# A two-layer decoder trunk: q, k and v of the attention layer in blocks of 512 columns, one block of tokens after the other, instead of units of 256 columns for both blocks at once

## The chip, the cores and the metric

The kernel runs on one core of one Trainium2 chip. The metric is the device time of one execution in microseconds. The kernel before was run three times: 932.15, 935.91 and 936.04 us, median 935.91 us. One more execution was recorded by the profiler.

## The reference

The input is one sequence of 256 tokens with 1024 features, in float32. Two layers follow each other. Only the first half of layer 0, its attention, is touched by the change:

```python
qkv = (h @ w_qkv).reshape(B, S, 3 groups, 3 (q, k, v), 16 heads, 64)    # h = rms_norm(x)
q = rms_norm(qkv[:, :, :, 0], q_gain)      # per head, over its 64 features
k = rms_norm(qkv[:, :, :, 1], k_gain)
v = qkv[:, :, :, 2]
for each group g with (window, dilation) in (128, 1), (512, 4), (2048, 16):
    s   = q . k * scale - slope * distance     # causal, keys gathered by stride
    lse = logsumexp(s);  out_g = exp(s - lse) . v
o = sum over groups of softmax(lse)_g * out_g
x = x + o @ w_o
```

After it come a squared-ReLU MLP (1024 to 4096 to 1024), an embedding gate, and layer 1: an mLSTM mixer, another MLP and another gate. The projection to q, k and v has 9216 output columns: 3 groups times (q, k, v) times 16 heads of 64.

## The kernel before, in words

**Weights.** All weights come as a stream of units, arrays of [128, 2048] float32 (1 MB). `dma(u)` loads unit u into one of three raw buffers from SyncE's queue. Float32 precision is reached with three products of a faster 32-bit type: each weight chunk of 512 columns is split into a high part `hi` (a rounding copy on ScalarE, L166) and a low part `lo` (raw minus hi on VectorE, L167), the activations are split in the same way (`hh`, `hl`), and each product is made as hi·hh + lo·hh + hi·hl, three matmuls into one sum. There are 12 chunk buffers each for `hi` and `lo`, which is three units.

**Slots.** A unit is worked off in four slots. `open_slot` issues the load of the unit four ahead at the first slot of a unit, and the splits of weight chunks up to `LS` = 11 slots ahead; `close_slot` calls what was registered for this slot with `at(slot, f, ...)`, the small work that is strewn between the stream's matmuls. From the code written in this order a scheduler with priorities makes the final order of each engine; splits are written at a lower priority (`BACK`), so that they move behind other work.

**q, k, v.** There are 36 units: for each quarter `qt` (four heads), for each group `g`, one unit each for q, k and v (`ty` 0, 1, 2). A unit holds 8 k-tiles of 256 columns. The activations are the stationary operand: for each k-tile and each block `b` of 128 tokens there are three matmuls of 128x256 (L474, L475, L476), so 12 matmuls in a slot, 48 in a unit and 1728 in all. The two token blocks lie side by side in one bank of 512 columns in `acc`.

**Norms of q and k.** After a q or k unit `qk_stats` squares the bank on ScalarE (`sqh`, L417) and sums over the 64 features of a head on VectorE (`ss`, L423, two instructions). After the k unit `qk_norm` makes 1/rms by an iteration of small VectorE instructions (`vqk` L427, then ten on `fqk` and `rt`, L267 to L271) and scales the sums into `n0` and `n1` (L435, four instructions). `TQ` = 5 and 6 slots later `qk_turn` transposes them on TensorE (L445, four each into `tp`), and ScalarE copies them out as `t0g` (q) and `t1g` (k), with a low part for group 0 on VectorE. So a turn of q stands behind the following v unit's four slots and one more. The second norm of the program is that of group 1 of quarter 0.

**Attention.** After the nine units of a quarter `attend` registers the quarter's attention from one slot later on: `scores` (L509 for group 0, L515 for groups 1 and 2) into `sc`, softmax on VectorE and ScalarE (L522 to L530), `turn` (L534) and `values` (L552, L556), with a step of `ST0` = 4 slots, and `ST1` = 1 for the last quarter, which falls into the stream that follows (`proj`, L317 to L319).

**The start.** x is loaded in four pieces between the pieces of the first two units. `first_stats` (L366, L368 and the iteration at L267 to L271) computes the norms of the tokens of x; some small products of the mLSTM's block matrices (`contract`, L397 to L404) run on GpSimd as soon as their input `rep` has come.

Of the kernel before, what the change touches and what calls it, by code (L numbers as in the profile page):

```python
# [32 lines left out]
# token order of layer 0: position a*64 + b*16 + c holds token 16c + 4b + a,  # L33
# which makes every class of a dilation (mod 4, mod 16) a run of positions
# [4 lines left out]

def _blocks(no, ks, singles=0):  # L40
    """outputs worked on together (k outermost): pairs, the last ones alone"""
    n = no - singles
    os = [(o, o + 1) for o in range(0, n, 2)] + [(o,) for o in range(n, no)]
    return [(b, list(ks)) for b in os]

# [57 lines left out]
def _consts():  # L103
# [5 lines left out]
    # columns: all keys for group 0; the keys of the row's class mod 4 for groups 1 and 2  # L109
    # (2 and 1 in the odd classes)  # L110
# [19 lines left out]
def _build(ctx, tc, nc, a):  # L130
# [45 lines left out]
    LS, LD = 11, 4  # L176
    fill = {}
    clock = [0]
    ahead = [7]
    LV = 6  # L180
# [5 lines left out]
    # slots after z0: the gates' steps; the start of a head, and its steps after that  # L186
    GT, HS, HO = (4, 6, 7), (6, 12, 18, 24), (0, 2, 5, 7)
    ST0 = 4
    ST1 = 1
    TQ = 5  # L190
# [35 lines left out]
    # the tensor engine's clock rises only after some time of work  # L226
# [11 lines left out]
    class Stats:  # L238
        """sum over features of x^2 -> per token"""
# [47 lines left out]
    def rstd_rows(st, power):  # L287
        """1/rms (power 1) or its square (power 2), on every partition"""
# [15 lines left out]
    def stream(blocks, rhs, done, defer=0):  # L304
        """acc[o] = sum over k of W[k, o]^T act[k]; done(outputs, acc) after every block"""
# [26 lines left out]
    # ================= layer 0: attention =================  # L332
# [47 lines left out]
    # small products of the mLSTM's block matrices  # L380
# [6 lines left out]
    def small_products():  # L387
# [4 lines left out]
        def contract(out, w, name, n, add=None):  # L392
# [22 lines left out]
    def qk_stats(qt, g, ty, acc):  # L415
        sq = atp.tile([P, 2, 4, HD], F32, name="sqh")
        act(sq, acc.rearrange("p b (h d) -> p b h d", d=HD), AF.Square)  # L417
        if ty == 0:
            STAT["ss"] = atp.tile([P, 2, 2, 4], F32, name="ss", bufs=2)
            STAT["q"] = acc  # L420
        ss = STAT["ss"]
        for b in range(2):
            dve.tensor_reduce(ss[:, b, ty], sq[:, b], axis=AX.X, op=ALU.add)  # L423

    def qk_norm(qt, g, accq, acck, ss):
        v = atp.tile([P, 2, 8], F32, name="vqk", bufs=2)
        dve.scalar_tensor_tensor(v, ss.rearrange("p b t h -> p b (t h)"), 1.0 / HD,  # L427
                                 epsx[:, :, None].to_broadcast([P, 2, 8]), op0=ALU.mult, op1=ALU.add)
        f = atp.tile([P, 2, 8], F32, name="fqk", bufs=2)
        rsqrt(f, v, [P, 2, 8])  # L430
        out = []
        for ty, acc in ((0, accq), (1, acck)):
            n = atp.tile([P, 2, 256], F32, name=f"n{ty}")
            for b in range(2):
                dve.tensor_tensor(n[:, b].rearrange("p (h d) -> p h d", d=HD),  # L435
                                  acc[:, b].rearrange("p (h d) -> p h d", d=HD),
                                  f[:, b, 4 * ty:4 * ty + 4, None].to_broadcast([P, 4, HD]), op=ALU.mult)
            out.append(n)
        return out

    def qk_turn(qt, g, ty, n):
        ps = pst.tile([P, 2, S], F32, name="tp")
        for pair in range(2):
            for b in range(2):
                nc.tensor.transpose(ps[:, pair, b * P:(b + 1) * P], n[:, b, pair * P:(pair + 1) * P], ident)  # L445
# [14 lines left out]
    def qkv_unit(qt, g, ty):  # L460
        if qt == 0 and ty == 0:
            acc = pss.tile([P, 2, 256], F32, name="sc")
        else:
            acc = psa.tile([P, 2, 256], F32, name="acc")
        for c in range(4):
            u, _ = open_slot()
            for k in (2 * c, 2 * c + 1):
                wh, wl = weights(u, k * 256, 256)
                for b in range(2):
                    if (g, ty) == (2, 2):  # L470
                        hh, hl = (t[:, k] for t in hW) if b else (t[:, k, 64:192] for t in hA)
                    else:
                        hh, hl = (t[:, k, b * P:(b + 1) * P] for t in hA)
                    mm(acc[:, b], hh, wh, start=(k == 0 and b == 0), stop=False, skip_group_check=True)  # L474
                    mm(acc[:, b], hh, wl, start=False, stop=False, skip_group_check=True)  # L475
                    mm(acc[:, b], hl, wh, start=False, stop=(k == 7), skip_group_check=True)  # L476
            if c == 3:
                if ty < 2:
                    qk_stats(qt, g, ty, acc)
                if ty == 1:  # L480
                    n = qk_norm(qt, g, STAT["q"], acc, STAT["ss"])
                    at(clock[0] + TQ, qk_turn, qt, g, 0, n[0])
                    at(clock[0] + TQ + 1, qk_turn, qt, g, 1, n[1])
                if ty == 2:
                    if g == 0:
                        VT[qt, 0] = atp.tile([P, 2, 256], F32, name="v0", bufs=2)
                    if g == 1:
                        VT[qt, 1] = atp.tile([P, 4, 256], F32, name="v12", bufs=2)
                    for b in range(2):
                        if g == 0:  # L490
                            act(VT[qt, 0][:, b], acc[:, b], AF.Copy, scale=rx[:, b:b + 1])
                            continue
                        c = 2 * b + (g == 2)
                        for r, c4 in ((slice(0, 64), c), (slice(64, 128), (c + 1) % 4)):
                            n = b + 2 * (g == 2)
# [559 lines left out]
```

## Time and profile before

| what | value |
|---|---|
| time, median of 3 | 935.91 us |
| span of the profiled execution | 933.2 us (what lies around the span isn't recorded) |
| TensorE busy | 917.9 us, 98% |
| VectorE busy | 664.5 us, 71% |
| ScalarE busy | 570.8 us, 61% |
| GpSimd busy | 41.6 us, 4% |
| DMA | 150.35 MB, mean 161 GB/s |
| chain that ended last | TensorE 92%, VectorE 5%, ScalarE 1%, DMA 1% |

The span goes from the first to the last instruction of the profiled execution. Engines are PE (TensorE matmuls), PEld (its weight loads, which overlap the matmuls), DVE (VectorE), ACT (ScalarE), POOL (GpSimd) and SP (SyncE). A matmul's record lasts longer than the time until the next one starts, since matmuls are pipelined; the pace is read from start to start. The first matmul of q, k and v starts 6.74 us after the span's start, the last one at 267.55 us, and the first matmul of the next stream (`proj`) at 273.46 us; what follows is 660 us long and isn't touched by the change, except that line numbers move by 14 or so.

### The profile page before, as it was taken

How to read it: one execution, taken by the hardware profiler on the slowest of the kernel's cores; microseconds unless marked ns; L12 is line 12 of the kernel's file. 1: busy time of each engine (PE TensorE's matmuls, PEld its weight loads, DVE VectorE, ACT ScalarE, POOL GpSimd, SP SyncE). 2: the span in 40 equal slices, each digit the busy share in tenths (PEclk: the TensorE clock that was granted, in tenths of full speed). 3: DMA queues.
4: the chain of work that ended last, by engine and by line, in shares of the span. 5: the costliest groups of instructions: out<-in, count | busy, mean ns of one | idle time of the engine just before them, and what ended most of it. 6: DMA issues, size and time to landing. Idle time of an engine off the chain costs nothing.

```text
span 933.2 us, 19379 instructions
## 1 busy us (share of the span) xinstructions
PE 917.9 (98%) x7788; PEld 899.8 (96%) x7788; DVE 664.5 (71%) x1457; ACT 570.8 (61%) x1055; POOL 41.6 (4%) x77
## 2 busy tenths in 40 slices
PE   8989999999999999999999999999999999999998
PEld 8989999999989999999999989999999999999997
DVE  6977767767756876665666987667898666656664
ACT  6646666666656666654554777668776666645542
POOL 0420000000000000000000153000000000000000
PEclk8999999999999999999999999999999999999999
DMA  8744334444342365555555343342356455555521
GB/s 297 267 144 173 136 137 139 145 165 142 137 147 92 137 211 188 186 183 182 181 181 182 131 151 136 112 147 80 115 176 211 176 182 185 187 183 185 186 105 46
DMA packets 23130, 150.35 MB, mean 161 GB/s; under 512 B 2560, under 2 KB 3200, under 8 KB 5632
## 3 DMA queue, kind: packets, MB, share of 16 engines
q1 hardware_dynamic: 23040, 149.12, 44.8%
q8 instruction: 61, 1.00, 0.4%
q14 instruction: 29, 0.24, 0.1%
HBM read 148.06 MB, written 1.05 MB: 160 GB/s over the span
## 4 chain that ended last, share of the span: by engine, by line
PE 92%; DVE 5%; ACT 1%; issue 1%; DMA 1%; SPq 0%; ACTq 0%
PE acc L317 21%; PE acc L318 20%; PE acc L319 20%; PE acc L474 6%; PE acc L475 6%; PE acc L476 6%; DVE lo L167 2%; PE tp L534 1%; PE sc L509 1%; PE tp L445 1%; PE sm L552 1%; PE sc L515 1%; PE tp L725 1%; PE tp L735 1%; PE sc L866 1%; PE sc L743 1%
## 5 line engine op out<-in xcount | busy, mean ns | idle before, releaser
L167 DVE TENSOR_TENSOR lo<-raw,hi 128x512 fp32r<-128x512 f32 x552 | 379.0, 693 | 184.5 <-ACT hi L166 182.3
L166 ACT ACTIVATE hi<-raw 128x512 fp32r<-128x512 f32 x552 | 341.9, 628 | 266.6 <-PE acc L318 208.8
L317 PE MATMUL acc<-hh,hi 128*128 128x256 f32 x640 | 184.0, 288 | 0.3 <-ACT hh L284 0.2
L318 PE MATMUL acc<-hl,hi 128*128 128x256 f32 x640 | 181.5, 284 | 0.1
L319 PE MATMUL acc<-hh,lo 128*128 128x256 f32 x640 | 181.4, 283 | 0.0
L474 PE MATMUL acc<-hi,hh 128*128 128x256 f32 x496 | 145.0, 292 | 0.0
L318 PE MATMUL acc<-hidl,hi 128*128 128x256 f32 x512 | 144.9, 283 | 0.0
L317 PE MATMUL acc<-hidh,hi 128*128 128x256 f32 x512 | 144.9, 283 | 0.0
L319 PE MATMUL acc<-hidh,lo 128*128 128x256 f32 x512 | 144.9, 283 | 0.0
L475 PE MATMUL acc<-lo,hh 128*128 128x256 f32 x496 | 140.3, 283 | 0.4 <-DVE lo L167 0.4
L476 PE MATMUL acc<-hi,hl 128*128 128x256 f32 x496 | 140.3, 283 | 0.0
L317 PEld LDWEIGHTS acc<-hh,hi 128*128 128x128 f32 x640 | 122.4, 191 | 1.5 <-issue 0.7
L318 PEld LDWEIGHTS acc<-hl,hi 128*128 128x128 f32 x640 | 122.4, 191 | 0.7 <-DVE hl L285 0.5
L319 PEld LDWEIGHTS acc<-hh,lo 128*128 128x128 f32 x640 | 122.4, 191 | 0.0
L317 PEld LDWEIGHTS acc<-hidh,hi 128*128 128x128 f32 x512 | 98.3, 192 | 0.0
L318 PEld LDWEIGHTS acc<-hidl,hi 128*128 128x128 f32 x512 | 98.3, 192 | 0.0
L319 PEld LDWEIGHTS acc<-hidh,lo 128*128 128x128 f32 x512 | 98.3, 192 | 0.0
L474 PEld LDWEIGHTS acc<-hi,hh 128*128 128x128 f32 x496 | 94.8, 191 | 1.4
L475 PEld LDWEIGHTS acc<-lo,hh 128*128 128x128 f32 x496 | 95.0, 191 | 0.6 <-DVE lo L167 0.6
L476 PEld LDWEIGHTS acc<-hi,hl 128*128 128x128 f32 x496 | 94.9, 191 | 0.0
L317 PE MATMUL acc<-hBh,hi 128*128 128x256 f32 x320 | 90.9, 284 | 0.0
L318 PE MATMUL acc<-hBl,hi 128*128 128x256 f32 x320 | 90.7, 283 | 0.0
(258 smaller groups left out, 1536.4 us busy)
## 6 DMA issues: line engine op xcount, KB each, us to landing
raw<-w SPq DMA_DIRECT2D x136, 1024.0 KB, 4.8
raw<-w SPq DMA_DIRECT2D x8, 256.0 KB, 7.2
x<-x SPq DMA_DIRECT2D x4, 256.0 KB, 5.7
pj<-rep SPq DMA_DIRECT2D x1, 896.0 KB, 6.6
out<-u SPq DMA_DIRECT2D x3, 256.0 KB, 2.6
pT<-p SPq DMA_DIRECT2D x2, 256.0 KB, 2.7
nd<-nd SPq DMA_DIRECT2D x1, 384.0 KB, 6.5
out<-u SPq DMA_DIRECT2D x2, 128.0 KB, 1.9
```

Of the source, the lines that this page charges most:

```text
L166: act(hi[n][:, d], raw[u][:, s], AF.Copy)
L167: dve.tensor_tensor(lo[n][:, d], raw[u][:, s], hi[n][:, d], op=ALU.subtract)
L317: mm(acc[:, q], wh, h, start=first, stop=False, skip_group_check=n > 1)
L318: mm(acc[:, q], wh, l, start=False, stop=False, skip_group_check=n > 1)
L319: mm(acc[:, q], wl, h, start=False, stop=last, skip_group_check=n > 1)
L445: nc.tensor.transpose(ps[:, pair, b * P:(b + 1) * P], n[:, b, pair * P:(pair + 1) * P], ident)
L474: mm(acc[:, b], hh, wh, start=(k == 0 and b == 0), stop=False, skip_group_check=True)
L475: mm(acc[:, b], hh, wl, start=False, stop=False, skip_group_check=True)
L476: mm(acc[:, b], hl, wh, start=False, stop=(k == 7), skip_group_check=True)
L509: mm(ps[:, 0:256], q[r, pair, tb], k[r, pair], start=first, stop=last)
L515: mm(ps[64 * e:64 * e + 64, 256 + 64 * n:320 + 64 * n], QT[qt, g][0][r, pair, t4], KTt[qt, g][0][r, pair, t4], start=True, stop=True)
L534: nc.tensor.transpose(psf[:, k * P:(k + 1) * P], pe[:, k * P:(k + 1) * P], ident)
```

## The change

The projection becomes 18 blocks of two units, eight slots each. For each quarter there are three blocks of q and k (one for each group: 256 columns of q beside 256 of k), then a block of v for groups 0 and 1, and in even quarters a block of v of group 2 for this quarter and the next. A unit now holds four k-tiles of 512 columns. A block goes through all eight k-tiles for token block 0 (slots 0 to 3), then again for token block 1 (slots 4 to 7); each token block has a PSUM bank of its own, and each matmul is 128x512. There are 864 of them in place of 1728.

The square and the sum of a token block follow right after its pass (24 reduces of 128x8 in place of 48 of 128x4), the norm after the second pass scales two tiles of 512 columns in place of four of 256. The turns stand `TQ` = 4 and 5 slots after the block's end. `attend` is registered at the beginning of the v block, to start 12 (even quarters) or 7 (odd quarters) slots after it, with a step of 3.5 slots. During q, k and v the splits run `LQ` = 7 slots ahead, then 11 as before, and within a slot they are issued ahead of the load. The GpSimd products sum in place. The tiles `n0` and `n1` are gone, whose memory `proj` used for its input p, so the load of p (256 KB) and its two copies stand some 30 loads further ahead in SyncE's, ScalarE's and VectorE's order.

```diff
-    LS, LD = 11, 4
+    LQ, LS, LD = 7, 11, 4
-    ST0 = 4
+    ST0 = 3.5
-    TQ = 5
+    TQ = 4
+    TA = (12, 7)
     def open_slot():
         u, c = divmod(clock[0], 4)
+        while ahead[0] < clock[0] + lead[0]:
+            ahead[0] += 1
+            split(*divmod(ahead[0], 4))
         if c == 0:
             dma(u + LD)
-        while ahead[0] < clock[0] + LS:
-            ahead[0] += 1
-            split(*divmod(ahead[0], 4))
...
-            s = atp.tile([P, 2, 16, 8], F32, name="cs")[:, :, :, :n]
             for j in range(2):
-                nc.gpsimd.tensor_tensor(s[:, j], t[:, :, :, j], t[:, :, :, j + 2], op=ALU.add)
-            nc.gpsimd.tensor_tensor(out, s[:, 0], s[:, 1], op=ALU.add)
+                nc.gpsimd.tensor_tensor(t[:, :, :, j], t[:, :, :, j], t[:, :, :, j + 2], op=ALU.add)
+            nc.gpsimd.tensor_tensor(out, t[:, :, :, 0], t[:, :, :, 1], op=ALU.add)
...
+    def qk_stats(b, acc):
+        sq = atp.tile([P, 8, HD], F32, name="sqh")
+        act(sq, acc.rearrange("p (h d) -> p h d", d=HD), AF.Square)
+        if b == 0:
+            STAT["ss"] = atp.tile([P, 2, 8], F32, name="ss", bufs=2)
+        dve.tensor_reduce(STAT["ss"][:, b], sq, axis=AX.X, op=ALU.add)
...
+    def qkv_block(qt, what, g):
+        u0 = clock[0] // 4
+        accs = []
+        for i in range(8):
+            open_slot()
+            for j in (2 * i, 2 * i + 1):
+                b, k = divmod(j, 8)
+                if k == 0:
+                    pl, nm = (pss, "sc") if qt == 0 and g == 0 and what == "qk" and b == 0 else (psa, "acc")
+                    accs.append(pl.tile([P, 512], F32, name=nm))
+                wh, wl = weights(u0 + k // 4, k % 4 * 512, 512)
...
+                mm(accs[b], hh, wh, start=(k == 0), stop=False)
+                mm(accs[b], hh, wl, start=False, stop=False)
+                mm(accs[b], hl, wh, start=False, stop=(k == 7))
+                if k == 7:
+                    if what == "qk":
+                        qk_stats(b, accs[b])
...
+            if i == 7 and what == "qk":
+                n = qk_norm(accs)
+                for ty in range(2):
+                    at(clock[0] + TQ + ty, qk_turn, qt, g, ty, n)
             close_slot()
...
-    for qt in range(4):
-        t1 = clock[0] + 36
-        for g in range(3):
-            for ty in range(3):
-                qkv_unit(qt, g, ty)
-        attend(qt, t1 + 1, ST0 if qt < 3 else ST1)
+    for qt, (what, g) in _qkv():
+        if (what, g) == ("v", 0):
+            attend(qt, clock[0] + TA[qt % 2], ST0 if qt < 3 else ST1)
+        qkv_block(qt, what, g)
+    lead[0] = LS
```

Three places of the final order. The first is VectorE at the second norm of the program (quarter 0, group 1). Before, both sums of squares `ss` stand ahead of the iteration, the splits between its steps, and the scaling to `n0` and `n1` at its end (`lo` is a weight split, `vqk`, `fqk` and `rt` are the iteration):

```order
L423 TENSOR_REDUCE ss_566<-sqh_636 128x4 x2
L167 TENSOR_TENSOR lo_621<-raw_478,hi_620 128x512
L427 SCALAR_TENSOR_TENSOR vqk_640<-ss_566,epsx_190 128x16
...
L270 SCALAR_TENSOR_TENSOR rt_643<-rt_643,vqk_640 128x16
L271 SCALAR_TENSOR_TENSOR fqk_642<-rt_643,fqk_642 128x16
L435 TENSOR_TENSOR n0_654<-sc_477,fqk_642 128x256 x2
L435 TENSOR_TENSOR n1_657<-acc_569,fqk_642 128x256 x2
```

Now (`ss_383` is the sum of this norm's second token block, `sqh_511` the square of the first token block of the block that follows, `nqk` the scaled q and k):

```order
L434 TENSOR_REDUCE ss_383<-sqh_448 128x8
L177 TENSOR_TENSOR lo_469<-raw_275,hi_468 128x512
L438 SCALAR_TENSOR_TENSOR vqk_451<-ss_383,epsx_190 128x16
...
L285 SCALAR_TENSOR_TENSOR fqk_453<-rt_454,fqk_453 128x16
L434 TENSOR_REDUCE ss_513<-sqh_511 128x8
L283 TENSOR_TENSOR rt_454<-fqk_453 128x16
...
L443 TENSOR_TENSOR nqk_465<-acc_340,fqk_453 128x512
L443 TENSOR_TENSOR nqk_465<-acc_400,fqk_453 128x512
```

In the middle of the iteration there is now a sum that reads a square of the next block; six small instructions and the two scalings stand behind it.

The second place is TensorE where this norm's result is turned. Before, the transposes (`tp_751`) stand behind the first slots of a later unit (`sc_732` is its sum):

```order
L474 MATMUL sc_732<-hi_505,hh_115 128x256
L475 MATMUL sc_732<-lo_506,hh_115 128x256
L476 MATMUL sc_732<-hi_505,hl_116 128x256
L445 MATMUL tp_751<-ident_84,n0_654 128x128 x4
L474 MATMUL sc_732<-hi_532,hh_115 128x256
```

Now they stand behind the last matmul of the next block's first pass (`acc_474`, whose square is `sqh_511`) and six matmuls of the first scores:

```order
L500 MATMUL acc_474<-lo_469,hh_115 128x512
L501 MATMUL acc_474<-hi_468,hl_116 128x512
L527 MATMUL sc_763<-t10h_412,t00h_390 128x256
L527 MATMUL sc_764<-t10h_412,t00h_390 128x256
...
L451 MATMUL tp_515<-ident_84,nqk_465 128x128
L499 MATMUL acc_528<-hi_351,hh_115 128x512
```

What TensorE has in hand between the last matmul on which the norm depends and its transposes is now those six score matmuls.

The third place is TensorE at the end of q, k and v. Before, the last eight transposes of q and k (`tp_3903`, `tp_3928`, of group 2 of the last quarter) stand directly ahead of the last quarter's first scores, which read their copies `t12h` and `t02h`:

```order
L445 MATMUL tp_3903<-ident_84,n0_3782 128x128 x4
L445 MATMUL tp_3928<-ident_84,n1_3785 128x128 x4
L509 MATMUL sc_3936<-t10h_3304,t00h_3279 128x256
...
L515 MATMUL sc_3936<-t11h_3641,t01h_3592 64x64
L515 MATMUL sc_3936<-t12h_3933,t02h_3908 64x64
```

Now matmuls of the last v block stand between them (`tp_2907` is the later of the two turns, `acc_2900` the block's second pass):

```order
L451 MATMUL tp_2907<-ident_84,nqk_2819 128x128 x4
L499 MATMUL acc_2900<-hi_2714,hh_115 128x512
...
L501 MATMUL acc_2900<-hi_2830,hl_116 128x512
L527 MATMUL sc_2948<-t10h_2583,t00h_2553 128x256
...
L533 MATMUL sc_2948<-t12h_2912,t02h_2892 64x64
```

Eighteen matmuls of 512 columns now stand between the last transposes and the scores that need them.

## Rows read from the trace of the kernel before

**Rows 1.** Page: the span of the profiled execution.
```profile
span 933.2 us, 19379 instructions
```

**Rows 2.** Stretches: start:end, us, busy us by engine, TensorE's granted clock, DMA, GB/s.
```profile
6.74:49.20 42.46, 41.55 (x315) 40.56 (x316) 38.14 (x89) 30.44 (x60) 12.36 (x16) 0.92 0.81 291
53.05:267.83 214.78, 214.66 (x2022) 207.96 (x2024) 154.93 (x442) 133.72 (x273) 0.00 (x0) 0.99 0.41 148
267.83:273.46 5.63, 4.02 (x55) 3.18 (x56) 3.39 (x10) 5.23 (x11) 0.00 (x0) 1.00 0.23 60
273.46:933.20 659.74, 653.19 (x5381) 644.08 (x5379) 462.62 (x903) 396.92 (x705) 26.01 (x52) 1.00 0.44 158
36.38:52.41 16.03, 13.10 (x110) 12.90 (x108) 15.82 (x29) 8.84 (x17) 15.40 (x21) 1.00 0.67 246
```

**Rows 3.** Timeline of TensorE: start us, us, engine, line, op, out<-in, shapes, count [idle before].
```profile
119.79 0.66 PE L445 MATMUL tp<-ident,n 128*128 128x128 f32 x4
...
120.40 0.28 PE L475 MATMUL acc<-lo,hh 128*128 128x256 f32 x1
...
123.04 0.28 PE L476 MATMUL acc<-hi,hl 128*128 128x256 f32 x1
```

**Rows 4.** Timeline of TensorE, near the start and in layer 1.
```profile
12.36 0.41 PE L474 MATMUL sc<-hi,hh 128*128 128x256 f32 x1
...
15.35 0.41 PE L476 MATMUL sc<-hi,hl 128*128 128x256 f32 x1
...
552.56 1.94 PE L743 MATMUL sc<-ut,xc 128*128 128x264 f32 x8
554.34 1.09 PE L745 MATMUL sc<-ut,xc 128*128 128x136 f32 x8
```

**Rows 5.** Timeline of VectorE and TensorE, behind the norms of x.
```profile
23.26 2.50 DVE L167 TENSOR_TENSOR lo<-raw,hi 128x512 fp32r<-128x512 f32 x4
```

**Rows 6.** Timeline of TensorE around its idle times in q, k and v.
```profile
49.20 0.28 PE L476 MATMUL sc<-hi,hl 128*128 128x256 f32 x1
53.05 1.14 PE L445 MATMUL tp<-ident,n 128*128 128x128 f32 x4 [3.56 <-DVE n L435]
...
56.55 0.62 PE L445 MATMUL tp<-ident,n 128*128 128x128 f32 x4
...
271.44 0.34 PE L515 MATMUL sc<-t12h,t02h 64*64 64x64 f32 x8 [0.96 <-ACT t12h L454]
...
272.54 0.38 PE L509 MATMUL sc<-t10h,t00h 64*128 64x256 f32 x1 [0.65 <-DVE m L522]
...
275.23 0.42 PE L319 MATMUL acc<-pT,lo 128*128 128x256 f32 x1
...
278.23 0.39 PE L319 MATMUL acc<-pT,lo 128*128 128x256 f32 x1
```

**Rows 7.** Timeline of ScalarE and VectorE: a norm in mid-stage.
```profile
108.37 0.57 ACT L417 ACTIVATE sqh<-acc 128x512 f32<-128x512 f32 x1
109.11 0.74 DVE L423 TENSOR_REDUCE ss<-sqh 128x4 f32<-128x256 f32 x2
...
110.37 0.17 DVE L427 SCALAR_TENSOR_TENSOR vqk<-ss,epsx 128x16 f32<-128x16 f32 x1
...
113.21 1.42 DVE L435 TENSOR_TENSOR n<-acc,fqk 128x256 f32<-128x256 f32 x4
114.54 1.28 DVE L167 TENSOR_TENSOR lo<-raw,hi 128x512 fp32r<-128x512 f32 x2
```

**Rows 8.** Timeline of VectorE at the second norm, and GpSimd's first product.
```profile
45.39 0.70 DVE L427 SCALAR_TENSOR_TENSOR vqk<-ss,epsx 128x16 f32<-128x16 f32 x1
...
48.89 0.64 DVE L271 SCALAR_TENSOR_TENSOR fqk<-rt,fqk 128x16 f32<-128x16 f32 x1
...
52.48 0.75 DVE L435 TENSOR_TENSOR n<-sc,fqk 128x256 f32<-128x256 f32 x2
...
36.38 1.24 POOL L397 TENSOR_TENSOR ct<-prm,pj 128x128 f32<-128x128 f32 x2 [35.94 <-DMA pj<-rep]
```

More of the change, by code (lines that the diff above doesn't have):

```diff
@@ L44, in _blocks, with _qkv @@
     return [(b, list(ks)) for b in os]
+def _qkv():
+    out = []
+    for qt in range(4):
+        out += [(qt, ("qk", g)) for g in range(3)] + [(qt, ("v", 0))]
+        if qt % 2 == 0:
+            out.append((qt, ("v", 2)))
+    return out
 def _tiles(blocks):
@@ L179, in _build @@
     ahead = [7]
+    lead = [LQ]
     LV = 6
@@ L413, in _build, with qk_norm @@
     STAT = {}
[L415 to L425, printed above, removed]
+    def qk_stats(b, acc):
[4 more added lines that the diff above has]
+        dve.tensor_reduce(STAT["ss"][:, b], sq, axis=AX.X, op=ALU.add)
+    def qk_norm(accs):
         v = atp.tile([P, 2, 8], F32, name="vqk", bufs=2)
-        dve.scalar_tensor_tensor(v, ss.rearrange("p b t h -> p b (t h)"), 1.0 / HD,
-                                 epsx[:, :, None].to_broadcast([P, 2, 8]), op0=ALU.mult, op1=ALU.add)
+        dve.scalar_tensor_tensor(v, STAT["ss"], 1.0 / HD, epsx[:, :, None].to_broadcast([P, 2, 8]), op0=ALU.mult, op1=ALU.add)
         f = atp.tile([P, 2, 8], F32, name="fqk", bufs=2)
         rsqrt(f, v, [P, 2, 8])
[L431 to L439, printed above, removed]
+        n = atp.tile([P, 2, 512], F32, name="nqk")
+        for b in range(2):
+            dve.tensor_tensor(n[:, b].rearrange("p (h d) -> p h d", d=HD), accs[b].rearrange("p (h d) -> p h d", d=HD),
+                              f[:, b, :, None].to_broadcast([P, 8, HD]), op=ALU.mult)
+        return n
     def qk_turn(qt, g, ty, n):
@@ L458, in qk_turn @@
         (QT if ty == 0 else KTt)[qt, g] = t
[L460 to L471, printed above, removed]
-                    else:
[L473 to L495, printed above, removed]
-                            act(VT[qt, 1][r, c4], acc[r, b], AF.Copy, scale=rx[r, n:n + 1])
@@ new lines, in v_tile, with v_out @@
+    def v_tile(qt, g):
+        n, c = (0, 2) if g == 0 else (1, 4)
+        if (qt, n) not in VT:
+            VT[qt, n] = atp.tile([P, c, 256], F32, name=f"v{n}", bufs=1 + n)
+        return VT[qt, n]
+    def v_out(qt, g, b, acc):
+        vt = v_tile(qt, g)
+        if g == 0:
+            act(vt[:, b], acc, AF.Copy, scale=rx[:, b:b + 1])
+            return
+        c = 2 * b + (g == 2)
+        n = b + 2 * (g == 2)
+        for r, c4 in ((slice(0, 64), c), (slice(64, 128), (c + 1) % 4)):
+            act(vt[r, c4], acc[r], AF.Copy, scale=rx[r, n:n + 1])
@@ new lines, in qkv_block @@
+    def qkv_block(qt, what, g):
[9 more added lines that the diff above has]
+                wh, wl = weights(u0 + k // 4, k % 4 * 512, 512)
+                if (what, g) == ("v", 2):
+                    hh, hl = (t[:, k] for t in hW) if b else (t[:, k, 64:192] for t in hA)
+                else:
+                    hh, hl = (t[:, k, b * P:(b + 1) * P] for t in hA)
+                mm(accs[b], hh, wh, start=(k == 0), stop=False)
[4 more added lines that the diff above has]
+                        qk_stats(b, accs[b])
+                    elif g == 0:
+                        v_out(qt, 0, b, accs[b][:, 0:256])
+                        v_out(qt, 1, b, accs[b][:, 256:512])
+                    else:
+                        v_out(qt, 2, b, accs[b][:, 0:256])
+                        v_out(qt + 1, 2, b, accs[b][:, 256:512])
+            if i == 7 and what == "qk":
+                n = qk_norm(accs)
+                for ty in range(2):
+                    at(clock[0] + TQ + ty, qk_turn, qt, g, ty, n)
@@ L572, in attend @@
         at(t0 + int(7 * step) + LV + 1, heads_done, qt)
-    for qt in range(4):
-        t1 = clock[0] + 36
-        for g in range(3):
-            for ty in range(3):
-                qkv_unit(qt, g, ty)
-        assert clock[0] == t1
-        attend(qt, t1 + 1, ST0 if qt < 3 else ST1)
+    for qt, (what, g) in _qkv():
[3 more added lines that the diff above has]
+    lead[0] = LS
     def proj(layer, p, tags):
@@ L984, in _layout @@
     units = []
-    for qt in range(4):
-        for g in range(3):
-            for ty in range(3):
-                units.append(qkv[:, :, g, ty, qt].transpose(1, 0, 2).reshape(P, UC))
+    for qt, (what, g) in _qkv():
+        if what == "qk":
+            two = (g, 0, qt), (g, 1, qt)
+        else:
+            two = ((0, 2, qt), (1, 2, qt)) if g == 0 else ((2, 2, qt), (2, 2, qt + 1))
+        w = np.concatenate([qkv[:, :, g, ty, q] for g, ty, q in two], 2)
+        for k in (0, 4):
+            units.append(w[k:k + 4].transpose(1, 0, 2).reshape(P, UC))
     wo = i["a_w_o"][0]
```

2 lines of the change are left out of this document (1 added, 1 removed).

## The prediction

> **What bounds the kernel now.** I read the share of busy time first (98% for TensorE in the table), then the stretches, then TensorE's timeline for its pace and its idle times, and last VectorE's timeline where TensorE waits for it. The stretches [rows 2] show TensorE busy for 214.66 of 214.78 us in the long middle of the q, k, v stage; there nothing else is worth looking at but its pace. Before that it is busy 41.55 of 42.46 us at a granted clock of 0.92, at the stage's end 4.02 of 5.63 us. The last row but one, 659.74 us, is untouched by the change, and I carry it over.
>
> What sets the pace? In mid-stage 22 matmuls of 256 columns start in 2.64 us, one every 0.120 us [rows 3]. At half the clock the same matmul starts every 0.2136 us (14 intervals in 2.99 us, rows 4), which is 256 columns at 1.2 GHz to the last digit. Were columns the limit at the full clock too, it would be 0.1067. So something else binds there, and the second row of the stretches names it: the weight loads, as many as the matmuls (2024 of them), are busy 207.96 of 214.78 us. A matmul that streams long enough pays only for its columns: in layer 1 eight float32 matmuls of 264 columns, two cycles a column as their time tells, start in 1.78 us, 222.5 ns each for 528 cycles (220 ns) and 2.5 ns beside [rows 4].
>
> **The change part by part.**
>
> *Pace.* 864 matmuls of 512 columns take the place of 1728 of 256, with the same columns and half the weight loads. No matmul of 512 such columns stands in the trace. From below it is 512 cycles, 213.3 ns; from above the pace per column stays, 240 ns. I take 213.3 + 2.5 = 216 ns from the row of 528 cycles, which is the nearest in length. 1728 x 0.120 - 864 x 0.216 = 20.7 us gained; matmuls at half the clock (some 48 of the 1728, where the columns bind already) gain nothing, so 20.1. Ends: 0 and 23.
>
> The Trainium skill, "TensorE: Matmul & The Clock Gate", section "Back-to-back issue gap", gives columns / 2.4 + 2.5 ns for one gap: 215.8 ns at 512 agrees with my value, but 109.2 ns at 256 does not agree with the 120 measured here, and by the rule alone the gain would be 864 x (218.4 - 215.8) = 2.2 us. The same section gives about 131 ns as the sustained time at 512, which would be a gain of 94 us; the 222.5 ns for 528 cycles speak against it.
>
> *The first stretch.* Before, TensorE loses three times. Behind the norms of x VectorE makes the next four low parts from 23.26 us on [rows 5], and TensorE waits some 0.6 us. The second norm's transposes start at 53.05 us, 3.85 us after the start of the matmul ahead of them, where one matmul takes 0.12: 3.7 lost [rows 6]. And after that the clock is at half: the four transposes and 12 matmuls from 53.05 to 56.55 us take 3.50 us, where in mid-stage four transposes take 0.41 (119.79 to 120.40, less one matmul of 0.2 behind them, rows 3) and 12 matmuls 1.44, so 1.65 lost. Together 5.9 us.
>
> That wait had a reason. In a quiet place a norm takes: square 0.57, sums 0.65, eleven small steps at 0.20 and one split (110.37 to 113.21), scaling 1.33 [rows 7]. In the second norm the same step lasts 0.70 and 0.64 in place of 0.17 [rows 8], and from 45.39 to 52.48 us it takes 7.1 us. GpSimd works there on its products, from 36.38 us on when their input lands [rows 8], 15.40 of 16.03 us, while VectorE is busy 15.82 of 16.03 [rows 2].
>
> Afterwards the same norm ends at a worse moment. The order shows a foreign sum, that of the next block's first pass, in the middle of its iteration; it cannot start before that pass is over, and directly behind this pass (and six score matmuls, some 0.6 us) stand the transposes. What TensorE then waits for is square, sum, six steps and two scalings: 0.57 + 0.65 + 1.2 + 1.33 and two hand-overs of 0.1 to 0.2, about 4.0 us in quiet and, with steps of 0.4 to 0.64 us, 5.5 to 6.7 beside GpSimd; less 0.6, it is 3.4 to 6.1. The pass ends about 23.3 + 0.7 + 12 slots of 1.296 = 39.6 us, so beside GpSimd. I take 5.0, and 1.65 for the clock, which fell after the 3.7 us before. Block 0 carries the like of it in small (its scaling stands behind the next block's first sum, but the two passes are interleaved there): 0.55. The wait behind the norms of x becomes 1.3, since a pass over one token block uses up a chunk in 0.65 us, about as fast as VectorE makes one (0.60 to 0.64, rows 5 and 7), and 0.4 more follow at that speed; the third norm's turn, with no scores ahead of it, 0.4. Sum 9.3, so 3.4 us lost. Ends: 1 us gained (no foreign wait at all) and 7 lost.
>
> The Trainium skill, "GPSIMD Engine Reference", section 1 "Specifications", says that GpSimd's interfaces to on-chip memory are shared with VectorE, which contends above all with two operands there. The trace agrees (0.70 against 0.17 us). It speaks against this change, which leaves the products in the same place and gives the norm's tail less cover; by it alone the wait would lie at the 6.1 of my bounds.
>
> *The end of the stage.* Before, TensorE waits 0.96 us for the copies of the last q and k, then 0.65 for the softmax's first row, and runs at half the clock later (275.23 to 278.23 us: 14 intervals of 0.214, rows 6), which costs again 1.6. Now 18 matmuls, 3.9 us, stand between the last transposes and the scores that need them, and the scores are followed by the stream. All 3.2 go. The splits' lead rises from 7 to 11 slots there, so four chunks are asked for at once, 2.5 us of VectorE in a row beside the softmax: 1 us lost. Gain 2.2; ends 3.2 gained, 1 lost.
>
> *Mid-stage norms.* Nine more norms follow. Each turn stood behind about five slots, 7.2 us of matmuls; now it stands behind the next block's first pass, 24 x 0.216 = 5.2 us and what attention work lies there (0.3 to 1.1). The quiet norm is 0.57 + 0.65 + 2.2 + 1.33 + a split of 0.6 and hand-overs, 5.6 us. The cover is just about gone, so some turns are late by up to half a microsecond. The splits, too, have less time: a first pass uses up all eight chunks of its block in 5.2 us, and VectorE needs 4.8 for eight; they are asked for seven slots ahead. I take 1.5 us over all; ends 0 and 13 (0.7 a block over 18 blocks).
>
> *What hides.* 24 sums and 24 scalings go from VectorE, which is 72% busy in mid-stage (154.93 of 214.78): 0 from that, since TensorE doesn't wait there. The in-place sums on GpSimd, the single buffer of `v0` and the earlier load of p (a quarter of a unit; DMA is at 0.41 in mid-stage) cost nothing while TensorE is fed. p's load comes right behind that of the tenth unit, where the first stretch's DMA share of 0.81 still holds, and its two copies of some 0.6 us go to a ScalarE and a VectorE that are full there; what that delays is a split that VectorE makes again in 0.6 us. It is in the upper bound of the first stretch.
>
> Sum: -20.1 + 3.4 - 2.2 + 1.5 = -17.4 us. The profiled span is 933.2 us [rows 1], so 915.8 for it; the median of the runs lies 2.7 above that span, which I keep: 918.5.
>
> **Rivals.**
>
> 1. The 120 ns are not weight loads but a price per column at this clock, and 512 columns take 240. For it: no row shows 512 columns of this type. Against it: the float32 matmuls at 222.5 ns for 528 cycles, and weight loads busy at 97%. Then 0 + 3.4 - 2.2 + 1.5 = +2.7, 938.6 us.
>
> 2. Every turn of q and k stalls as the second norm's did before. The mechanism: VectorE's chain ends after the one pass that is now its cover, TensorE idles at the transposes (in its queue the second pass, whose bank the scaling also has to release, stands behind them), and the clock falls. Price 3.7 + 1.65 = 5.3 each; 12 of them 64 us, so -20.1 - 2.2 + 64 = +42, 977 us. It decides against the change from (20.1 + 2.2) / 12 = 1.9 us a norm on. For it: cover 5.2 to 6.3 against a chain of 5.6, any softmax step or split in the chain makes it late. Against it: the quiet rows, and that VectorE has 28% of its time free there.
>
> 3. In between: turns late by 1 us on average, through splits and softmax steps in the chain, without a fall of the clock: 12 us, 930.5 us in all less the 1.5 already counted, 929.0.
>
> **How the numbers follow.** The forecast gets 0.71 (with its own terms it lies between 908 and 927), rival 3 0.13, rival 1 0.09, rival 2 in full or half strength 0.07. Half a per cent, 4.7 us, is about what a measurement of this kernel can tell from no change. Faster by more than that, under 931.2: 0.71 and most of rival 3, 0.82. Within: the rest of rival 3 and most of rival 1, 0.11. Slower: 0.07. Low end: 23.0 gained in pace, the early waits cut by 1, 3.2 at the end, with the median 908.5; high end 932, which takes in rival 3 with its spread and leaves out rivals 1 and 2 in 0.16.
>
> **What would show it.** Right: matmuls of 512 columns start every 0.216 us in mid-stage; the stage from first to last matmul shrinks from 260.8 us to some 245; one idle time of 3.4 to 6 us at the second norm's transposes, put down to VectorE's scaling, and half the clock behind it; no waits between the last transposes and the first `proj` matmuls. Wrong: a pace of 0.24; idle times of over 1.9 us at transposes in every quarter; TensorE waiting for low parts in the first passes.

## The result

The changed kernel takes 921.91 us (median of 4 runs, 921.63 to 921.99); in the same comparison the kernel before takes 934.59 us. The ratio is 0.9861 (95% interval 0.9839 to 0.9884), a gain of 12.7 us where 17.4 was forecast. The median of the kernel before moved between 934.6 and 935.8 us from one comparison to the next, so a single difference of about 1 us is not told from none. The profiled execution has a span of 919.9 us against 933.2 [rows 1], 13.3 us less.

The stretches of the changed kernel, with the columns of [rows 2]: the stage's start up to the second norm, the long middle, from the last matmul of q, k, v to the first of the next stream, the rest, and the time in which GpSimd works.

```profile
6.94:39.59 32.65, 31.80 (x141) 25.32 (x142) 30.29 (x75) 24.55 (x48) 4.43 (x7) 1.00 0.83 314
44.89:260.39 215.50, 215.09 (x1353) 171.66 (x1354) 157.08 (x408) 141.72 (x292) 3.36 (x6) 0.99 0.43 148
260.39:261.65 1.26, 1.26 (x24) 0.74 (x22) 1.26 (x3) 1.26 (x3) 0.00 (x0) 1.00 0.64 104
261.65:919.90 658.25, 651.62 (x5395) 642.53 (x5388) 464.26 (x908) 398.32 (x707) 28.62 (x52) 1.00 0.47 160
34.93:48.44 13.51, 8.49 (x40) 6.66 (x39) 11.05 (x23) 3.48 (x7) 12.65 (x21) 0.87 0.65 229
```

From the first to the last matmul of q, k, v it is 253.5 us (6.94 to 260.39) in place of 260.8: 7.4 us, where some 15 were expected. From there to the next stream it is 1.26 us in place of 5.9 (267.55 to 273.46): 4.65 us, of which some 1.8 are sums of v and transposes (267.76 to 269.60 us before) that have moved into the stage. The rest, 658.25 against 659.74 us [rows 2], gives another 1.5: the stretch at half the clock behind the stage's end [rows 6] is gone. The weight loads, busy for 97% of the long middle before, are busy for 80% of it now (171.66 of 215.50 us).

TensorE's timeline in the long middle, start and duration in us:

```profile
61.67 0.39 PE L500 MATMUL acc<-lo,hh 128*128 128x512 f32 x1
...
71.43 0.39 PE L501 MATMUL acc<-hi,hWl 128*128 128x512 f32 x1
```

Between these two rows lie 43 intervals in 9.76 us: a matmul of 512 columns starts every 0.227 us, not 0.216. Over all undisturbed intervals of the stage the mean is 0.2291 (in some stretches it is 0.231), before 0.1197 for 256 columns, so 1728 x 0.1197 - 864 x 0.2291 = 8.9 us.

TensorE around the second norm and at the end of the stage, the places of [rows 6]:

```profile
39.59 0.28 PE L527 MATMUL sc<-t10h,t00l 64*128 64x256 f32 x2
44.89 0.45 PE L451 MATMUL tp<-ident,nqk 128*128 128x128 f32 x1 [5.02 <-DVE nqk L443]
...
45.56 0.63 PE L500 MATMUL acc<-lo,hh 128*128 128x512 f32 x1
45.98 0.63 PE L501 MATMUL acc<-hi,hl 128*128 128x512 f32 x1
...
260.71 0.39 PE L527 MATMUL sc<-t10h,t00h 64*128 64x256 f32 x2
...
261.65 0.39 PE L331 MATMUL acc<-pT,hi 128*128 128x256 f32 x1
261.88 0.28 PE L332 MATMUL acc<-pT,hi 128*128 128x256 f32 x1
```

The wait of 5.0 us at the second norm's transposes is there as forecast, and the clock is at half behind it (0.42 from start to start at 45.56), for some 3 us, which costs about 1.3 (44.89 to 47.86 us for work that takes some 1.66 at the pace of the rows behind it). At the end nothing waits any more, and the next stream begins 0.94 us after the first score. VectorE in the second norm, beside the places of [rows 8]:

```profile
38.34 0.70 DVE L283 TENSOR_TENSOR rt<-fqk 128x16 f32<-128x16 f32 x1
38.96 0.68 DVE L177 TENSOR_TENSOR lo<-raw,hi 128x512 fp32r<-128x512 f32 x1
39.56 0.68 DVE L284 SCALAR_TENSOR_TENSOR rt<-rt,vqk 128x16 f32<-128x16 f32 x1
40.17 0.68 DVE L177 TENSOR_TENSOR lo<-raw,hi 128x512 fp32r<-128x512 f32 x1
40.77 0.38 DVE L285 SCALAR_TENSOR_TENSOR fqk<-rt,fqk 128x16 f32<-128x16 f32 x1
41.07 0.67 DVE L434 TENSOR_REDUCE ss<-sqh 128x8 f32<-128x512 f32 x1
41.67 0.35 DVE L283 TENSOR_TENSOR rt<-fqk 128x16 f32<-128x16 f32 x1
...
44.05 1.29 DVE L443 TENSOR_TENSOR nqk<-acc,fqk 128x512 f32<-128x512 f32 x2
```

No row has idle time before it. The foreign sum at 41.07 follows the step ahead of it at once: its input, squared from 39.70 us on, had been there for 0.8 us.

### The profile page after: what moved, and what is told of

Read it like the earlier page. It is cut to its first block, busy times and chain, and to the rows that moved or that the text cites. A ratio compares the mean times of both kernels' runs of the same rounds, so it can differ in the third digit from the quotient of the medians.

```text
span 919.9 us, 17609 instructions
## 1 busy us (share of the span) xinstructions
PE 904.3 (98%) x6924; PEld 844.3 (92%) x6924; DVE 659.7 (72%) x1409; ACT 569.5 (62%) x1055; POOL 41.5 (5%) x77
## 4 chain that ended last, share of the span: by engine, by line
PE 92%; DVE 6%; ACT 1%; issue 1%; DMA 0%; SPq 0%; ACTq 0%
PE acc L331 21%; PE acc L332 21%; PE acc L333 21%; PE acc L499 6%; PE acc L501 6%; PE acc L500 6%; DVE lo L177 2%; PE tp L451 1%; PE tp L552 1%; PE sm L570 1%; PE sc L527 1%; PE tp L741 1%; PE tp L751 1%; PE sc L882 1%; PE sc L759 1%; PE sc L533 1%
## 5 line engine op out<-in xcount | busy, mean ns | idle before, releaser
L499 PE MATMUL acc<-hi,hh 128*128 128x512 f32 x264 | 109.6, 416 | 0.0
L500 PE MATMUL acc<-lo,hh 128*128 128x512 f32 x264 | 104.1, 394 | 0.8 <-DVE lo L177 0.8
L501 PE MATMUL acc<-hi,hl 128*128 128x512 f32 x264 | 104.2, 395 | 0.0
L333 PE MATMUL acc<-hBh,lo 128*128 128x256 f32 x320 | 90.6, 283 | 0.0
L331 PEld LDWEIGHTS acc<-hBh,hi 128*128 128x128 f32 x320 | 61.4, 192 | 0.3 <-issue 0.3
L332 PEld LDWEIGHTS acc<-hBl,hi 128*128 128x128 f32 x320 | 61.4, 192 | 0.0
```

What stands on the lines that cost most here:

```text
L331: mm(acc[:, q], wh, h, start=first, stop=False, skip_group_check=n > 1)
L332: mm(acc[:, q], wh, l, start=False, stop=False, skip_group_check=n > 1)
L333: mm(acc[:, q], wl, h, start=False, stop=last, skip_group_check=n > 1)
L499: mm(accs[b], hh, wh, start=(k == 0), stop=False)
L500: mm(accs[b], hh, wl, start=False, stop=False)
L501: mm(accs[b], hl, wh, start=False, stop=(k == 7))
```

## The experiments

All times are medians; a difference is taken to the changed kernel's 921.9 us, and each ratio is to the kernel before, run beside it.

**The width alone.** `e1_halves`:

```diff
-                mm(accs[b], hh, wh, start=(k == 0), stop=False)
-                mm(accs[b], hh, wl, start=False, stop=False)
-                mm(accs[b], hl, wh, start=False, stop=(k == 7))
+                for c in range(2):
+                    w2 = slice(256 * c, 256 * c + 256)
+                    mm(accs[b][:, w2], hh, wh[:, w2], start=(k == 0 and c == 0), stop=False, skip_group_check=True)
+                    mm(accs[b][:, w2], hh, wl[:, w2], start=False, stop=False, skip_group_check=True)
+                    mm(accs[b][:, w2], hl, wh[:, w2], start=False, stop=(k == 7), skip_group_check=True)
```

> The changed kernel with every matmul of 512 columns cut into two of 256, and nothing else. Theory A (the pace is a price per matmul: columns at 2.4 GHz and some 13 ns more, 0.1195 us for 256 and 0.2275 for 512): the gaps go back to 0.1195 to 0.12, 864 x 0.0115 = 9 to 10 us are given back, 931 us. Rival (the gain came from the order of the work at the start, at the second norm and at the end, and the width matters little): 922 to 925 us.

929.05 us, ratio 0.9937 (0.9922 to 0.9951): 7.1 us given back. The mean interval is 0.1197 us again. So the width carries 7 us, a little under the 8.9 of the intervals. Why a little under isn't shown: in this kernel's profile the second norm's wait is 1 us shorter (4.0 us), but TensorE runs at half the clock behind it for 4.5 us (45.99 to 50.51) in place of 2.9. Between 5 and 6 us of the gain come from elsewhere.

**What a matmul of each width costs.** `p1_widths`, one execution (937.04 us), read for the pace alone:

```diff
+    CUT = {(1, "qk", 0): (384, 128), (1, "qk", 1): (128,) * 4, (1, "qk", 2): (256, 256), (2, "qk", 0): (320, 192)}
...
```

> The changed kernel, where quarter 1 cuts its matmuls of group 0 into 384 and 128 columns, of group 1 into four of 128, of group 2 into two of 256, and quarter 2 those of group 0 into 320 and 192; read for the pace alone. Theory A (columns at 2.4 GHz and some 13 ns for each matmul): 384 columns start every 0.173, 320 every 0.146, 256 every 0.1195, 192 every 0.0935 or at a floor of some 0.11 that the weight loads set. Theory W (of the prediction: the weight load of 0.12 or the columns and 2.5 ns, whichever is longer): 384 every 0.1625, 320 every 0.136, 192 and 128 every 0.12.

TensorE's timeline in the cut blocks:

```profile
92.26 0.34 PE L505 MATMUL acc<-lo,hh 128*128 128x384 f32 x1
92.43 0.34 PE L506 MATMUL acc<-hi,hl 128*128 128x384 f32 x1
92.61 0.22 PE L504 MATMUL acc<-hi,hh 128*128 128x128 f32 x1
92.67 0.27 PE L505 MATMUL acc<-lo,hh 128*128 128x128 f32 x1
92.79 0.27 PE L506 MATMUL acc<-hi,hl 128*128 128x128 f32 x1
92.90 0.40 PE L504 MATMUL acc<-hi,hh 128*128 128x384 f32 x1
93.13 0.34 PE L505 MATMUL acc<-lo,hh 128*128 128x384 f32 x1
...
107.75 0.27 PE L505 MATMUL acc<-lo,hh 128*128 128x128 f32 x1
...
108.86 0.28 PE L506 MATMUL acc<-hi,hl 128*128 128x128 f32 x1
...
148.37 0.31 PE L505 MATMUL acc<-lo,hh 128*128 128x320 f32 x1
148.51 0.31 PE L506 MATMUL acc<-hi,hl 128*128 128x320 f32 x1
148.66 0.25 PE L504 MATMUL acc<-hi,hh 128*128 128x192 f32 x1
148.75 0.27 PE L505 MATMUL acc<-lo,hh 128*128 128x192 f32 x1
148.86 0.27 PE L506 MATMUL acc<-hi,hl 128*128 128x192 f32 x1
```

| columns | measured (median) | columns at 2.4 GHz | over it |
|---|---|---|---|
| 128 | 0.111 | 0.053 | 0.058 |
| 192 | 0.113 | 0.080 | 0.033 |
| 256 | 0.120 | 0.1067 | 0.013 |
| 320 | 0.146 | 0.1333 | 0.013 |
| 384 | 0.1745 | 0.160 | 0.0145 |
| 512 | 0.227 | 0.2133 | 0.0137 |

The medians leave out the first matmul of a width after another width, whose next start is shifted: a wide one behind narrow ones is followed after 0.233 us (384) or 0.169 (320), a narrow one behind wide ones after 0.060 (128) or 0.088 (192), so that about what the one is over its median the other is under it.

From 256 columns on, a matmul of this type costs its columns and 13 to 14 ns. In series, 128 and 192 columns take nearly the same, 0.111 and 0.113 us, so there is a floor that doesn't go by columns and that a matmul of 256 columns (0.120) does not touch; one weight load for each matmul would explain it, which was not tried apart. Theory W is refuted: it wanted 0.1625 at 384, 0.136 at 320 and 0.12 at 192 and 128.

**The foreign sum.** `e2_one_buffer`:

```diff
-            STAT["ss"] = atp.tile([P, 2, 8], F32, name="ss", bufs=2)
+            STAT["ss"] = atp.tile([P, 2, 8], F32, name="ss", tag="ssf")
...
-        f = atp.tile([P, 2, 8], F32, name="fqk", bufs=2)
+        f = atp.tile([P, 2, 8], F32, name="fqk", tag="ssf")
```

> The sums of squares and the iterate share one buffer, so that the next block's first sum can only stand behind this norm's scalings. Theory of the prediction (the foreign sum holds the second norm up until the next pass is over): the wait at the second norm's transposes falls from 5.0 us to about 1, and the time by 4, to 918. Rival (VectorE has no idle time in that norm, so the foreign sum costs only its own 0.6 us): 5.0 becomes 4.4, and the time stays within 1 us.

920.91 us, ratio 0.9855 (0.9838 to 0.9872), no change that can be told from none; the wait is 4.08 us in place of 5.02:

```profile
44.95 0.44 PE L451 MATMUL tp<-ident,nqk 128*128 128x128 f32 x1 [4.08 <-DVE nqk L443]
```

The theory, which wanted a wait of about 1 us and 918, is refuted, and the rival's numbers hold within the scatter: the sum costs little more than its own time. In three kernels below whose order up to this norm is the changed kernel's on every engine (`e7_late_turn`, `e10_p_late`, `e11_turn_and_p_late`) the profiles show 5.01 to 6.23 us, so a difference of 1 us in it is not told from none either.

**GpSimd.** `e3_no_products` (the products left out) and, as a kernel that computes everything, `e8_late_products`, where a first tiny operation makes them wait for a late tile:

```diff
-        for n, c in enumerate(((mcomp, wq, "wkr", 4), (wgX, wq, "g0", 8), (t2, wk, "g1", 8, wgX), (wgM, wv, "g2", 8))):
-            at(clock[0] + 4 * n + 1, contract, *c)
+        for t in (mcomp, wgX, wgM):
+            dve.memset(t, 0.0)
```
```diff
...
+            if after is not None:
+                nc.gpsimd.tensor_tensor(t[:, 0, 0, 0:1], after, after, op=ALU.mult)
...
-        for n, c in enumerate(((mcomp, wq, "wkr", 4), (wgX, wq, "g0", 8), (t2, wk, "g1", 8, wgX), (wgM, wv, "g2", 8))):
+        for n, c in enumerate(((mcomp, wq, "wkr", 4, None, KTt[0, 2][0][:, 0, 0:1]), (wgX, wq, "g0", 8), (t2, wk, "g1", 8, wgX), (wgM, wv, "g2", 8))):
```

> GpSimd's products are left out and their results filled with zeros, so what layer 1 computes is not the reference's. Theory (GpSimd slows VectorE's steps): the small steps of the second norm go back from 0.27 to 0.70 us to 0.2, the norm ends some 2.5 to 3 us earlier, the wait falls from 5.0 to 2 to 2.5, and the time by 2.5 to 4 with the clock behind it (the later GpSimd work of layer 1 stays). Rival (it is the five splits between the steps): the wait stays at 4.5 or more.

> GpSimd's products wait for the last copy of the third turn and so run from about 62 to 76 us, where no norm follows for 16 slots. Nothing is left out. If GpSimd's share in the second norm's wait is what leaving out the products showed (2 us of time), 920 us; if the products cost as much at the new place (splits and the first softmax there are slowed and TensorE waits for them), 921 to 923.

919.96 us (0.9842, 0.9828 to 0.9856) and 920.40 us (0.9837, 0.9819 to 0.9855). The wait is 3.14 and 3.15 us:

```profile
42.49 0.30 PE L451 MATMUL tp<-ident,nqk 128*128 128x128 f32 x1 [3.14 <-DVE nqk L443]
```
```profile
43.06 0.45 PE L453 MATMUL tp<-ident,nqk 128*128 128x128 f32 x1 [3.15 <-DVE nqk L445]
```

Some 2 us of the 5 are GpSimd's, less than the 2.5 to 3 that were expected. VectorE in `e3_no_products`:

```profile
38.23 0.17 DVE L284 SCALAR_TENSOR_TENSOR rt<-rt,vqk 128x16 f32<-128x16 f32 x1
38.31 0.69 DVE L177 TENSOR_TENSOR lo<-raw,hi 128x512 fp32r<-128x512 f32 x1
38.91 0.17 DVE L285 SCALAR_TENSOR_TENSOR fqk<-rt,fqk 128x16 f32<-128x16 f32 x1
39.81 0.69 DVE L434 TENSOR_REDUCE ss<-sqh 128x8 f32<-128x512 f32 x1 [0.73 <-ACT sqh L431]
40.41 0.17 DVE L283 TENSOR_TENSOR rt<-fqk 128x16 f32<-128x16 f32 x1
```

The steps take 0.17 us again. And now the foreign sum does wait, 0.73 us for the square: without GpSimd VectorE gets there before the pass is over. In late products GpSimd works from 60.24 us on, but for one instruction at 34.86, and no wait of TensorE over 0.2 us appears there.

**More work in hand.** `e4_banks`:

```diff
-                    pl, nm = (pss, "sc") if qt == 0 and g == 0 and what == "qk" and b == 0 else (psa, "acc")
+                    pl, nm = (pss, "sc") if qt == 0 and what == "qk" and b == 0 else (psa, "acc")
```

> In quarter 0 the first pass of all three blocks of q and k goes into a bank of the scores' pool (before, only the first block's). The second pass then needs no bank that the norm still holds, and the order puts some twenty more matmuls ahead of the second norm's transposes, 4.5 us less the six score matmuls that move away. Theory (a lack of cover): the wait of 5.0 us falls to 1 to 1.5 and the time by 3.5 to 5, to about 917.5. Rival (VectorE is behind with everything there, and TensorE waits for low parts instead): 921 to 922.

919.97 us, ratio 0.9843 (0.9828 to 0.9857), 1.9 us gained, and a wait of 2.89 us is left where 1 to 1.5 was expected:

```profile
48.72 0.41 PE L451 MATMUL tp<-ident,nqk 128*128 128x128 f32 x2 [2.89 <-DVE nqk L443]
```

The transposes moved back from 44.89 to 48.72 us: VectorE's end came later too, because ten splits now stand between the sum and the scalings where five stood. Half of the cover was eaten by work that slipped into the gaps between its steps.

**The end of the stage.** Three kernels: the last turn five slots later (`e7_late_turn`), p loaded into a buffer that is free only after the last transposes (`e10_p_late`), and both, which comes near the order of before at this place (`e11_turn_and_p_late`):

```diff
-                    at(clock[0] + TQ + ty, qk_turn, qt, g, ty, n)
+                    at(clock[0] + TQ + ty + (5 if (qt, g) == (3, 2) else 0), qk_turn, qt, g, ty, n)
...
-            attend(qt, clock[0] + TA[qt % 2], ST0 if qt < 3 else ST1)
+            attend(qt, clock[0] + (TA[qt % 2] if qt < 3 else 9), ST0 if qt < 3 else ST1)
```
```diff
-    prep, ph = proj(0, atp, ("n0", "n1", "sqh"))
+    prep, ph = proj(0, atp, ("nqk", "n1", "sqh"))
```

> The changed kernel with the last turn of q and k (group 2 of the last quarter) five slots later, so that its eight transposes stand behind the last matmul of q, k, v, and the last attention two slots later, as before. p is loaded early, as in the changed kernel. Theory A (what was won at the end of the stage is the place of the last turn): 2.5 to 4 us are given back, 925. Theory B (it is the early load of p, which lets the next stream's matmuls fill in around the turn): within 1 us of the changed kernel.

> The changed kernel with p loaded into the buffer of the scaled q and k, so that its load waits for the last transposes, as before; the turns stay early. Theory A: no change, under 1 us, as the transposes are over 3.9 us earlier than the scores. Theory B: the first matmul of the next stream comes later than the scores, by the load (2.7 us) and two copies less what the last pass covers, 1 to 2 us given back.

> Both: the last turn behind the last matmul and p loaded after it, which is the order of the kernel before at this place. Theory A: as with the late turn alone. Theory B: only the two together open the wait, 4 to 5 us given back with the half clock behind it, 926 to 927.

923.87 (0.9875, 0.9857 to 0.9892), 922.70 (0.9867, 0.9849 to 0.9886) and 929.29 us (0.9930, 0.9913 to 0.9948): 2.0, 0.8 and 7.4 us given back. Not all of that lies at the end. The fifth block (v of group 2, quarters 0 and 1) stands behind the second norm and far ahead of the places that were edited; its first matmul in the changed kernel and in these three, in this order:

```profile
64.85 0.39 PE L499 MATMUL acc<-hi,hh 128*128 128x512 f32 x1
```
```profile
66.24 0.39 PE L499 MATMUL acc<-hi,hh 128*128 128x512 f32 x1
```
```profile
67.39 0.39 PE L499 MATMUL acc<-hi,hh 128*128 128x512 f32 x1
```
```profile
64.69 0.39 PE L499 MATMUL acc<-hi,hh 128*128 128x512 f32 x1
```

From there to the end of the span (919.9, 922.1, 922.4 and 925.8 us) it is 855.0, 855.9, 855.0 and 861.1 us: the late turn alone costs 0.8 us, the late p nothing, both 6.1. What else the medians show stands ahead of the fifth block, where one and the same order gives different times: the wait at the second norm is 5.05 us in `e7_late_turn` and 6.23 in `e10_p_late`, and the half clock behind it takes 4.7 and 5.7 us of TensorE's work in place of 2.9. In `e10_p_late` the end is as in the changed kernel (score at 263.30, next stream at 264.25 us). So at the end Theory B holds for the late turn, Theory A for the late p, and Theory B for both, with a price set too low: either edit alone costs next to nothing, and only the two together open the wait. TensorE's end of the stage with both:

```profile
262.25 0.34 PE L533 MATMUL sc<-t12h,t02h 64*64 64x64 f32 x8 [0.84 <-ACT t12h L460]
...
263.35 0.38 PE L527 MATMUL sc<-t10h,t00h 64*128 64x256 f32 x1 [0.65 <-DVE m L540]
...
266.19 0.65 PE L331 MATMUL acc<-pT,hi 128*128 128x256 f32 x3 [0.35 <-ACT pT L606]
...
269.12 0.41 PE L333 MATMUL acc<-pT,lo 128*128 128x256 f32 x1
```

The same two waits as before [rows 6] are back, then one for p's copy, and then half the clock (0.41 us rows from 267.41 to 273.39 us; by the granted clock 6.8 us, where before it was 3.4, so that these two edits undo some 1.5 us more than the change had won there). SyncE issued p's load at 260.63 us here. In the kernel before it was issued, and p copied on ScalarE, at these times:

```profile
269.27 0.33 SPq L586 DMA_DIRECT2D pT<-p  x1
```
```profile
272.16 0.63 ACT L590 ACTIVATE pT<-pT 128x512 fp32r<-128x512 f32 x1
```

In the changed kernel p's load is issued at 41.26 us. With p there, in the late turn alone, 24 matmuls of the next stream fill in ahead of the turns and between them (261.11 to 264.41 us) and the longest wait is 0.20:

```profile
261.11 0.28 PE L331 MATMUL acc<-pT,hi 128*128 128x256 f32 x1
...
266.33 0.34 PE L533 MATMUL sc<-t12h,t02h 64*64 64x64 f32 x8 [0.20 <-ACT t12h L460]
```

**Both causes undone.** `e13_halves_end_late`: the edits of the halves, the late turn and the late p.

> Halves of 256 columns, the last turn late and p late, together: the two causes undone at once. Theory (width and end of the stage are all of the gain, each worth what it was worth alone: 7.1 and 7.4 us): 936, the time of the kernel before within 2 us, a little above it because the second norm's wait stays. Rival (a third part of the change, such as fewer instructions on VectorE, carries some of it, or the two overlap): 930 to 933.

934.33 us against 934.85 for the kernel before, ratio 0.9993 (0.9980 to 1.0007). With width and end of the stage undone nothing measurable of the gain is left. In the medians the two seem to overlap by 2 us (7.1 + 7.4 against 12.4); in the traces, from the fifth block on, they hardly do: 6.0 and 6.1 us alone, 11.6 together. What the change wins and loses at the start was not undone; that it cancels to within 2 us is all that this run shows of it.

**All remedies together.** `e9_best`: late products, the scores' bank, one buffer.

> Late products, the scores' bank for the first passes of quarter 0, and one buffer for sums and iterate, together; nothing is left out. If the second norm's wait is the end of VectorE's queue against what TensorE has in hand: quiet steps bring it from 5.3 to 3.4 (as seen with late products), the foreign sum 1.4 less, and the bank gives TensorE some 4 us of matmuls, so no wait above 0.5 us and no half clock behind it; 921.9 - 5 - 1.2 = 915 to 916.5. Rival (VectorE only takes more splits in between, as with the bank alone): a wait of 2 to 3 us is left, 919.

915.81 us (915.56 to 916.04), ratio 0.9786 (0.9773 to 0.9800), 6.1 us better than the changed kernel, 19 to 20 better than the kernel before. Its TensorE at the place of the second norm:

```profile
43.29 0.39 PE L501 MATMUL acc<-hi,hh 128*128 128x512 f32 x1
43.57 0.41 PE L453 MATMUL tp<-ident,nqk 128*128 128x128 f32 x2
43.73 0.48 PE L502 MATMUL acc<-lo,hh 128*128 128x512 f32 x1
```

No wait and no half clock; the longest wait left in the stage behind its start is 0.81 us at a softmax step. Each remedy alone gave 1 to 2 us and left a wait of 2.89 to 4.08 us with a stretch at half the clock behind it; together they gave 6 and left neither.

## Why the prediction was right, and where it was not

The range held the time and the direction was right; not every step was.

- **Pace: mis-sized.** The forecast was 20.1 us, the intervals show 8.9, and undoing the width costs 7.1. The step that failed is "216 ns from the row of 528 cycles". That row belongs to plain float32 matmuls of two cycles a column; the type used here costs 13 to 14 ns a matmul over its columns, not 2.5. The reading that "something else binds there", the weight loads, failed with it: weight loads busy 97% of the time were a sign of one load for each matmul, not of a bound. Had 0.120 been read as 0.1067 + 0.0133, the sum would have been 864 x 0.0133 = 11.5 us. Rival 1, a price per column, is refuted as well: it wanted 0.24.

The Trainium skill, "TensorE: Matmul & The Clock Gate", section "Back-to-back issue gap", adds 2.5 ns to the columns and also states some 131 ns at 512 and 81 at 128 for a sustained stream. The runs show 227 and 111; for this type the formula is 11 ns short, and the sustained figures don't hold.

- **Second norm: right in size, wrong in what held VectorE.** 5.0 us were forecast and measured; since profiles of the same order show 5.0 to 6.2, so close a hit is luck. What the forecast listed behind the foreign sum was there (six steps and two scalings, the sum starting at 41.07 us, the scalings at 44.05). But the foreign sum did not hold VectorE up: VectorE was full throughout, with GpSimd's slowing (2 us, by leaving it out) and splits between the steps. The foreign sum's wait appears only once GpSimd is out of the way (0.73 us). The 1.65 for the clock was some 1.3.

The Trainium skill, "GPSIMD Engine Reference", section 1 "Specifications", names the interfaces shared with VectorE; by that rule, moving the products had to shorten the steps. The trace agrees: 0.17 us without them, up to 0.70 beside them.

- **End of the stage: right cause, mis-sized.** 2.2 us were forecast. Undoing it costs 7.4 us in the medians and 6.1 from the fifth block on, of which some 1.5 are the longer half clock; some 4.5 remain (an estimate), and 4.65 + 1.5 less the 1.8 of moved work, 4.3, says the same. The earlier turn does take the waits away, as forecast. The terms that failed are the 1 us set aside for splits, for which TensorE did not wait, and "the earlier load of p ... cost nothing": its cost is nothing that shows, but its gain was not asked for. Before, p's copy began at 272.16 us, so until then the next stream could not fill TensorE's waits for scores, and the clock fell behind them. With p at hand even the late turn costs only 0.8. In the forecast's sum the half clock's 1.6 is also too much for its own rows: 14 x (0.214 - 0.120) is 1.3.

- **Mid-stage norms: no wait.** 1.5 us were set aside; after the second norm no wait of TensorE in the stage is over 0.25 us in the trace; the one at a softmax step (203.71 us) is 0.22. Rival 2, every turn stalling, is refuted, and rival 3 with it.

- **The start.** The wait for low parts behind the norms of x is 0.8 us (1.3 expected in all), and the waits forecast for the first norm (0.55) and the third (0.4) did not come. How long q, k and v run at half the clock at the start, by the pace of the rows, differs between profiles of kernels with the same start (0 to 3.8 us), so nothing is made of the shorter stretch in the changed kernel's (3.3 us, where before it was 6.8).

The misses partly cancelled: 11 us too much for the pace against some 2 too little at the end, 1.5 us of mid-stage waits that did not come, and, as what is left of the sum, some 2 to 3 us less lost at the start. That the time came out 3.4 us from the forecast is in part luck.

## What to carry to other kernels

Fit a price to two widths before naming the bound: an engine that is busy all the time may only be keeping step, and a row of another data type prices that type. When buffers are freed, ask which waiting load starts earlier and what that lets begin, not only what it costs; and where two edits each take the same wait away, undo both before calling either the cause. Where several engines' lateness ends at one wait, removing one cause shows only the next one; test the remedies together before dropping any.

## What the runs showed of the hardware

- A matmul of this 32-bit type costs, at 2.4 GHz, its columns plus 13 to 14 ns between 256 and 512 columns (0.120, 0.146, 0.1745, 0.227 us), with a floor of 0.111 to 0.113 us at 128 and 192. At 1.2 GHz nothing is added: 0.2136 us for 256 columns [rows 4] and 0.427 for 512. What the 13 ns are was not tried.
- In some stretches of the stage the 512-column interval is 0.231 in place of 0.227 us. What makes the difference stays open.
